# A gradient along rows: in-place tiles of one row per partition, six buffers, loads and stores in a fixed alternating order

## The chip, the cores and the metric

The kernel runs on one core of one Trainium2 chip; the other cores are idle. The metric is the device time of one execution in microseconds (us); less is better. All runs quoted here were in the fast state, with a granted clock of 1.0. A ratio is the mean time of one kernel's fast runs over the mean time of the fast runs of the kernel before from the same rounds, so it is not quite the ratio of the medians beside it. Ratios carry a 95% interval.

## The reference

```python
def setup_inputs():
    return {"x": np.random.randn(8192, 8192).astype(np.float32)}   # seeded

def reference(x):
    return np.gradient(x, axis=1)
```

Inside a row the result is `(x[j+1] - x[j-1]) / 2`; at its two ends it is the plain difference of neighbours. There is almost no arithmetic: 268.44 MB are read and 268.44 MB are written.

## The kernel before

A set is 256 rows, two consecutive rows for each of the 128 partitions of SBUF, the memory on the chip that the engines compute in. One load brings a set, 8 MB, into one of two buffers. Each of the two rows goes through a subtraction on VectorE (DVE) into an output tile, a multiplication by 0.5 on ScalarE (ACT), and a 4 MB store. All transfers are issued on the queue of SyncE (SP). The last set is cut into quarters, so that its first store can start early.

```python
    R = 2
    ...
    x_sets = x.rearrange("(s p t) m -> s p t m", p=P, t=R)
    out_sets = out.rearrange("(s p t) m -> s p t m", p=P, t=R)
    xpool = ctx.enter_context(tc.tile_pool(name="xpool", bufs=2))   # 2 x 64 KB per partition
    opool = ctx.enter_context(tc.tile_pool(name="opool", bufs=2))   # 2 x 32 KB per partition

    for i in range(nsets):                                          # 32 sets
        x_tile = xpool.tile([P, R, m], x.dtype)
        nc.sync.dma_start(out=x_tile, in_=x_sets[i])                # L32
        nchunks = 4 if i == nsets - 1 else 1
        for t in range(R):
            o_tile = opool.tile([P, m], out.dtype)
            for c in range(nchunks):
                ...
                nc.vector.tensor_sub(out=o_tile[:, lo:hi], ...)     # L45
                ...                                                 # first and last column
                nc.scalar.mul(out=o_tile[:, lo:hi], in_=o_tile[:, lo:hi], mul=0.5)          # L62
                nc.sync.dma_start(out=out_sets[i, :, t, c0:c1], in_=o_tile[:, c0:c1])       # L67
```

## Time and profile before

Three runs took 1255.21 us in the median (1253.86 to 1257.19). What matters of the profile:

| | kernel before |
|---|---|
| span of the profiled run | 1256.6 us |
| DMA engines, share of 40 slices | 9 tenths or more in 39 of them |
| mean rate, reads and writes together | 427 GB/s |
| DVE, ACT busy | 45%, 36% |

The lines come from the profile page: busy time by engine, the 40 slices, the chain that ended last, the two costliest groups (line, engine, operation, output<-input, count, busy us, mean ns, idle time before them), and the transfers with their median time from issue to landing.

```profile
DVE 565.4 (45%) x198; ACT 452.3 (36%) x71; POOL 0.2 (0%) x4
...
DMA  9999999999999999999999999999999999999997
GB/s 405 430 430 434 438 432 432 423 433 432 441 434 416 429 432 444 434 423 423 433 443 432 430 425 431 435 441 430 423 433 436 441 427 425 428 432 428 434 412 308
...
DMA 58%; DVE 23%; ACT 18%; issue 0%; DVEq 0%
...
L45 DVE TENSOR_TENSOR o_tile<-x_tile 128x8190 f32<-128x8190 f32 (+2 forms) x70 | 556.7, 7959 | 679.4 <-DMA out_dram<-o_tile 656.8
L62 ACT ACTIVATE o_tile<-o_tile 128x8190 f32<-128x8190 f32 (+2 forms) x70 | 451.0, 6443 | 793.6 <-DVE o_tile L45 793.6
...
out_dram<-o_tile SPq DMA_DIRECT2D x62, 4096.0 KB, 23.0
...
x_tile<-in_x_dram SPq DMA_DIRECT2D x32, 42.5
```

DVE stands idle for 679.4 us, nearly all of it waiting for stores to free an output tile. That looks like a cost, but the DMA row says otherwise: the transfer engines are busy throughout. A store lands 23.0 us after its issue, while moving 4 MB takes about 9.7 us; so when a store is issued, some 13 us of other work is still queued ahead of it. I call this number (landing time less transfer time) the queue ahead. It is a rough measure: a landing counts from the engine that ends last, so it also holds the lag of that engine and about a microsecond of start and completion.

Only at the end is there a weak place. The windows view gives, for stretches of 4 us, the busy time of DVE, ACT and POOL, the TensorE clock (of no use here), the DMA share and GB/s. Packets count where they start, so shares scatter around 1.

```profile
1220.00:1224.00 4.00, 0.00 (x0) 0.00 (x0) 0.00 (x0) 1.00 0.97 418
1224.00:1228.00 4.00, 1.96 (x1) 0.00 (x0) 0.00 (x0) 1.00 0.46 197
1228.00:1232.00 4.00, 4.00 (x4) 3.27 (x2) 0.00 (x0) 1.00 0.49 211
1232.00:1236.00 4.00, 3.36 (x4) 3.42 (x3) 0.00 (x0) 1.00 1.01 420
```

For about 7 us the DMA engines are half idle. The timeline (start, duration, engine and line) shows why: the last set's first subtraction waits for a store to free its output tile.

```profile
1226.04 2.29 DVE L45 TENSOR_TENSOR o_tile<-x_tile 128x2047 f32<-128x2047 f32 x1 [20.19 <-DMA out_dram<-o_tile]
```

The trace also records every DMA packet with start, duration and size, and I use sums of these records:

- **Nominal time**: every packet at its usual duration, 309 ns for 8 KB, 1213 ns for 32 KB, 2418 ns for 64 KB, summed and divided by 16 engines. For the kernel before it is 1240.4 us.
- **Stalls**: what packets took beyond that, divided by 16. Here 7.7 us, of which 6.4 us in the 64 KB packets, that is in the loads.
- **Idle at the end**: 16 less the number of data packets open, integrated over time and divided by 16, late in the run. Here 3.9 us in the hole and 3.1 us while the engines finish one after the other.
- **Spread**: for each transfer, the time from its first to its last completion count. The Trainium skill, page "DMA: Bandwidth & Descriptors", section "Why a DMA increments its semaphore by 16 and not by 1", says that a DMA runs on up to 16 engines that finish independently, and the semaphore counts them. The traces here agree: 16 counts arrive for each transfer.

### The profile page before, as it was taken

What the parts mean: (1) busy time and instruction counts of PE and PEld (TensorE: products, weight loads), DVE (VectorE), ACT (ScalarE), POOL (GpSimd) and SP (SyncE); (2) the same over time, 40 slices, a digit from 0 to 9 for tenths busy, and PEclk for the clock granted to TensorE, in tenths of its full rate; (3) what the DMA queues carried; (4) which work ended last, traced back from release to release, by engine and by line L of the source; (5) the groups of instructions that cost most, each with busy time, mean ns of one, the idle gap of its engine ahead of it and who ended that gap; (6) DMA issues with size and microseconds to landing.
All of it is one profiled execution on the core that took longest, in us unless ns stands there. A gap on an engine that the chain in (4) does not pass through costs nothing.

```text
span 1256.6 us, 670 instructions
## 1 busy us (share of the span) xinstructions
DVE 565.4 (45%) x198; ACT 452.3 (36%) x71; POOL 0.2 (0%) x4
## 2 busy tenths in 40 slices
DVE  2534553345533455334553345533455333554335
ACT  0434422344223442234422344223443234432244
POOL 0000000000000000000000000000000000000000
DMA  9999999999999999999999999999999999999997
GB/s 405 430 430 434 438 432 432 423 433 432 441 434 416 429 432 444 434 423 423 433 443 432 430 425 431 435 441 430 423 433 436 441 427 425 428 432 428 434 412 308
DMA packets 14693, 536.92 MB, mean 427 GB/s; under 512 B 1632, under 2 KB 1632, under 8 KB 1632
## 3 DMA queue, kind: packets, MB, share of 16 engines
q1 hardware_dynamic: 14688, 536.88, 99.4%
q14 instruction: 5, 0.04, 0.0%
HBM read 268.44 MB, written 268.44 MB: 427 GB/s over the span
## 4 chain that ended last, share of the span: by engine, by line
DMA 58%; DVE 23%; ACT 18%; issue 0%; DVEq 0%
DMA out_dram<-o_tile 57%; DVE o_tile L45 23%; ACT o_tile L62 18%; DMA x_tile<-in_x_dram 2%; DVEq L45 0%; DVE o_tile L57 0%; DVE o_tile L51 0%; DVEq L95 0%
## 5 line engine op out<-in xcount | busy, mean ns | idle before, releaser
L45 DVE TENSOR_TENSOR o_tile<-x_tile 128x8190 f32<-128x8190 f32 (+2 forms) x70 | 556.7, 7959 | 679.4 <-DMA out_dram<-o_tile 656.8
L62 ACT ACTIVATE o_tile<-o_tile 128x8190 f32<-128x8190 f32 (+2 forms) x70 | 451.0, 6443 | 793.6 <-DVE o_tile L45 793.6
L51 DVE TENSOR_TENSOR o_tile<-x_tile 128x1 f32<-128x1 f32 x64 | 9.8, 153 | 0.0
L57 DVE TENSOR_TENSOR o_tile<-x_tile 128x1 f32<-128x1 f32 x64 | 9.8, 153 | 0.0
L62 ACT ACT_TABLE_LOAD x1 | 1.3, 1283 | 0.7 <-PEq L84 0.7
L84 POOL MEMSET const-bfloat16-1.0<- 128x1 bf16 x1 | 0.1, 101 | 0.0
L84 POOL MEMSET const-uint8-127<- 128x1 uint8 x1 | 0.1, 101 | 0.0
L84 POOL MEMSET const-float32-0.0<- 128x1 f32 x1 | 0.1, 98 | 0.2 <-issue 0.2
L84 POOL MEMSET const-float32-1.0<- 128x1 f32 x1 | 0.1, 98 | 0.0
## 6 DMA issues: line engine op xcount, KB each, us to landing
out_dram<-o_tile SPq DMA_DIRECT2D x62, 4096.0 KB, 23.0
out_dram<-o_tile SPq DMA_DIRECT2D x8, 1024.0 KB, 8.1
x_tile<-in_x_dram SPq DMA_DIRECT2D x32, 42.5
```

The lines of the kernel that those rows point to most:

```text
L45: nc.vector.tensor_sub(out=o_tile[:, lo:hi], in0=x_tile[:, t, lo + 1 : hi + 1], in1=x_tile[:, t, lo - 1 : hi - 1],)
L51: nc.vector.tensor_sub(out=o_tile[:, 0:1], in0=x_tile[:, t, 1:2], in1=x_tile[:, t, 0:1],)
L57: nc.vector.tensor_sub(out=o_tile[:, m - 1 : m], in0=x_tile[:, t, m - 1 : m], in1=x_tile[:, t, m - 2 : m - 1],)
L62: nc.scalar.mul(out=o_tile[:, lo:hi], in_=o_tile[:, lo:hi], mul=0.5,)
L84: nc = _bacc.Bacc("TRN2", target_bir_lowering=False, num_devices=1)
```

## The change

Its intent: every tile is one row per partition (4 MB), computed in place, with the data loaded 64 elements above where the result goes. That makes room for six buffers. Loads run ahead in a fixed order that no scheduler alters: after store i comes load i+4, which waits for store i-2.

```diff
-    R = 2
+    R = 1
+    LAG, BACK = 6, 2
+    SH = 64
...
-    xpool = ctx.enter_context(tc.tile_pool(name="xpool", bufs=2))
-    opool = ctx.enter_context(tc.tile_pool(name="opool", bufs=2))
+    pool = ctx.enter_context(tc.tile_pool(name="pool", bufs=LAG))
...
+    def diff(b, c0, c1):
+        ...                                        # first and last column cut
+        nc.vector.tensor_sub(
+            out=b[:, lo:hi],
+            in0=b[:, SH + lo + 1 : SH + hi + 1],
+            in1=b[:, SH + lo - 1 : SH + hi - 1],
+        )
+        ...
+        nc.scalar.mul(out=b[:, lo:hi], in_=b[:, lo:hi], mul=0.5)
+    def load(i):
+        b = pool.tile([P, SH + W], x.dtype)
+        nc.sync.dma_start(out=b[:, SH : SH + W], in_=x_sets[i])
+        return b
+    with tc.manual_schedule():
+        held = [load(i) for i in range(LAG)]
+        for i in range(nsets):                     # 64 tiles
+            b = held[i]
+            last = i == nsets - 1
+            step = m // 4 if last else m // 2
+            for c0 in range(0, W, step):
+                diff(b, c0, c0 + step)
+                if last: ...                       # store this quarter
+            if not last:
+                nc.sync.dma_start(out=out_sets[i], in_=b[:, 0:W])
+            j = i - BACK
+            if j >= 0 and j + LAG < nsets:
+                held.append(load(j + LAG))
```

More of the change, by code (lines that the diff above doesn't have):

```diff
@@ L19 @@
     n, m = x.shape
-    R = 2
-    rows_per_set = P * R
-    nsets = n // rows_per_set
-    x_sets = x.rearrange("(s p t) m -> s p t m", p=P, t=R)
-    out_sets = out.rearrange("(s p t) m -> s p t m", p=P, t=R)
-    xpool = ctx.enter_context(tc.tile_pool(name="xpool", bufs=2))
-    opool = ctx.enter_context(tc.tile_pool(name="opool", bufs=2))
-    for i in range(nsets):
-        x_tile = xpool.tile([P, R, m], x.dtype)
-        nc.sync.dma_start(out=x_tile, in_=x_sets[i])
-        last = i == nsets - 1
-        nchunks = 4 if last else 1
-        for t in range(R):
-            o_tile = opool.tile([P, m], out.dtype)
-            csz = m // nchunks
-            for c in range(nchunks):
-                c0 = c * csz
-                c1 = c0 + csz
-                lo = max(c0, 1)
-                hi = min(c1, m - 1)
-                nc.vector.tensor_sub(
-                    out=o_tile[:, lo:hi],
-                    in0=x_tile[:, t, lo + 1 : hi + 1],
-                    in1=x_tile[:, t, lo - 1 : hi - 1],
-                )
-                if c0 == 0:
-                    nc.vector.tensor_sub(
-                        out=o_tile[:, 0:1],
-                        in0=x_tile[:, t, 1:2],
-                        in1=x_tile[:, t, 0:1],
-                    )
-                if c1 == m:
-                    nc.vector.tensor_sub(
-                        out=o_tile[:, m - 1 : m],
-                        in0=x_tile[:, t, m - 1 : m],
-                        in1=x_tile[:, t, m - 2 : m - 1],
-                    )
-                nc.scalar.mul(
-                    out=o_tile[:, lo:hi],
-                    in_=o_tile[:, lo:hi],
-                    mul=0.5,
-                )
-                nc.sync.dma_start(
-                    out=out_sets[i, :, t, c0:c1], in_=o_tile[:, c0:c1]
-                )
@@ new lines @@
+    R = 1
+    LAG, BACK = 6, 2
+    SH = 64
+    W = R * m
+    nsets = n // (P * R)
+    x_sets = x.rearrange("(s p t) m -> s p (t m)", p=P, t=R)
+    out_sets = out.rearrange("(s p t) m -> s p (t m)", p=P, t=R)
+    pool = ctx.enter_context(tc.tile_pool(name="pool", bufs=LAG))
+    def diff(b, c0, c1):
+        lo, hi = c0, c1
+        if c0 % m == 0:
+            lo = c0 + 1
+            nc.vector.tensor_sub(
+                out=b[:, c0:lo],
+                in0=b[:, SH + c0 + 1 : SH + c0 + 2],
+                in1=b[:, SH + c0 : SH + c0 + 1],
+            )
+        if c1 % m == 0:
+            hi = c1 - 1
+        nc.vector.tensor_sub(
+            out=b[:, lo:hi],
+            in0=b[:, SH + lo + 1 : SH + hi + 1],
+            in1=b[:, SH + lo - 1 : SH + hi - 1],
+        )
+        if hi < c1:
+            nc.vector.tensor_sub(
+                out=b[:, hi:c1],
+                in0=b[:, SH + hi : SH + c1],
+                in1=b[:, SH + hi - 1 : SH + c1 - 1],
+            )
+        nc.scalar.mul(out=b[:, lo:hi], in_=b[:, lo:hi], mul=0.5)
@@ new lines, in load @@
+    def load(i):
[10 more added lines that the diff above has]
+                diff(b, c0, c0 + step)
+                if last:
+                    nc.sync.dma_start(
+                        out=out_sets[i, :, c0 : c0 + step], in_=b[:, c0 : c0 + step]
+                    )
+            if not last:
[3 more added lines that the diff above has]
+                held.append(load(j + LAG))
```

## The prediction

> **What bounds the kernel now.** The DMA engines. The page's DMA row is 9 in every one of 40 slices but the last (7), at a mean of 427 GB/s over 1256.6 us. DVE is busy 45%, ACT 36%. The chain of waits names stores (58%), L45 (23%) and L62 (18%), but that is the chain through small buffer pools, not idle DMA: DVE waits 656.8 us for stores while the queue still holds work. Counting the trace's packet records, 16 are open at every moment from first to last data packet, except near the end.
>
> The packets' durations give the ceiling: 64 KB in 2418 ns, 32 KB in 1213, 8 KB in 309: 27.2 GB/s per engine plus about 8 ns a packet, or 432 to 434 GB/s on 16 engines. The Trainium skill, page "DMA: Bandwidth & Descriptors", section "Where 436 GB/s comes from", states 435.2 GB/s as the fabric's ceiling; this trace agrees within 1%. 536.87 MB must move either way. To be had are only:
> - stalls of packets beyond these durations: 7.7 us per engine, 6.4 of them in 64 KB loads;
> - a hole before the last set, whose compute waits for a store (20.2 us at 1226 us): some 9 engines idle for 6.5 us, 3.7 us on average;
> - an uneven end, about 3 us on average (one engine ends 3.7 us after most);
> - start and completion, 1.7 us each.
>
> **What the change does.**
> - Loads become 4 MB in 32 KB rows: 4096 packets of 64 KB become 8192. Estimate from the durations: +8 ns x 4096 / 16 = +2.1 us; fewer 8 KB packets at the end give back 0.3 to 0.5.
> - The first compute starts after 4 MB (about 11 us, not 22.5). Worth nothing: the queue is full of loads then.
> - Load i+4 waits only for store i-2, with about four transfers of 9.7 us queued behind that store (before, 14 to 24 us of queue were left). As the queue never ran dry, no gain in the steady part.
> - At the end, stores 60 to 62 (29 us) follow load 63 and hide the last tile's compute. The hole goes; but the lagging engines, which set the end, hardly waited in it: 0.5 to 3.5 us gained.
> - DVE and ACT work in halves (about 4.4 and 3.6 us): 12.4 us a tile from landing to result, against 19.4 us of DMA per tile. Hidden.
>
> **Sum.** +1.7 for packets, -0.5 to -3.5 at the end, stalls as before: about 1 us less. I predict 1254 us, range 1248 to 1260; within 2% 0.95; faster by over 2% 0.02 (the data alone take about 1238 us); slower by over 2% 0.03.
>
> **What would show it.**
> - DMA row 9 to the end, mean 427 to 431 GB/s; the last two slices above 412 and 308; 32 KB packets still at about 1213 ns.
> - No hole before the last tile.
> - DVE's waits for stores replaced by waits for loads, 650 to 690 us in total, worth nothing. Loads take about 50 us to land, stores 50 to 56 (before 42.5 and 23): a deeper queue.
> - DVE and ACT busy as before within 3%.
>
> **What would make it wrong.** Loads and stores alternate every 4 MB instead of 8, and a deep queue lets engines drift apart: if mixed reads and writes stall packets more often, the 7.7 us grow (conceivably 1 to 2% slower); if 32 KB rows stall less, they shrink by up to 6 us. An engine that lags more, or less, moves the uneven end by a few us.

## The result, and the profile after

The changed kernel took 1252.07 us in the median (1251.22 to 1252.39, 4 runs) beside 1256.2 us for the kernel before in all its runs up to then (1253.86 to 1257.59, 4 runs). The ratio is 0.9968 (0.9949 to 0.9987): about 4 us, or 0.3%, faster. The same parts of the page:

```profile
DVE 587.1 (47%) x258; ACT 464.5 (37%) x131; POOL 0.2 (0%) x4
...
DMA  9999999999999999999999999999999999999998
GB/s 403 422 434 436 434 430 430 430 433 431 432 432 432 434 429 434 433 431 435 432 430 436 431 434 433 433 433 433 432 436 431 434 432 431 436 434 430 435 431 350
...
DMA 63%; another core or an unknown queue 18%; DVE 12%; ACT 5%; SPq 0%; issue 0%; DVEq 0%
...
L58 ACT ACTIVATE b<-b 128x4095 f32<-128x4095 f32 (+1 forms) x130 | 463.2, 3563 | 743.6 <-DVE b L47 743.6
L47 DVE TENSOR_TENSOR b<-b 128x4095 f32<-128x4095 f32 (+1 forms) x130 | 566.7, 4359 | 4.8 <-DVE b L40 0.3
L40 DVE TENSOR_TENSOR b<-b 128x1 f32<-128x1 f32 x64 | 10.2, 160 | 625.2 <-DMA b<-in_x_dram 625.2
...
b<-in_x_dram SPq DMA_DIRECT2D x64, 4096.0 KB, 48.4
out_dram<-b SPq DMA_DIRECT2D x63, 4096.0 KB, 55.0
```

DVE now waits for loads (625.2 us) and not for stores, and that is worth as little as before: its wait changed its name, not the time. A store lands 55.0 us after its issue, so the queue ahead of it grew from 13 to 45 us. (The 18% of the chain on "an unknown queue" are steps that this view could not attribute; nothing is read from it.) The GB/s row is more even: before, it swings between 416 and 444 in the steady part, now between 429 and 436 from the third slice on. The windows at the end:

```profile
1228.00:1232.00 4.00, 0.00 (x0) 0.00 (x0) 0.00 (x0) 1.00 0.97 418
...
1236.00:1240.00 4.00, 0.00 (x0) 0.00 (x0) 0.00 (x0) 1.00 0.98 414
1240.00:1244.00 4.00, 0.00 (x0) 0.00 (x0) 0.00 (x0) 1.00 0.81 340
1244.00:1248.00 4.00, 0.00 (x0) 0.00 (x0) 0.00 (x0) 1.00 0.19 82
```

The hole is gone; what is left is a ragged end, in which fewer and fewer engines have work. The sums over packet records, two profiles of each kernel (the second ones are the controls below):

| | before | before again | after | after again |
|---|---|---|---|---|
| span, us | 1256.6 | 1254.3 | 1249.4 | 1250.5 |
| data packets | 13056 | 13056 | 16768 | 16768 |
| nominal time, us | 1240.4 | 1240.4 | 1242.3 | 1242.3 |
| stalls, us per engine | 7.7 | 6.0 | 2.7 | 2.5 |
| idle, hole + ragged end, us | 3.9 + 3.1 | 3.4 + 3.0 | 0.0 + 3.9 | 0.0 + 5.1 |
| spread, us, at 300 / 600 / 1100 us | 5.1 / 8.9 / 11.7 | 3.5 / 6.4 / 10.0 | 4.1 / 5.5 / 5.5 | 5.5 / 6.5 / 6.5 |

(Spreads are means over the 100 us that begin there.) The mean span fell by 5.5 us. Stalls fell by 4.3 us (mean of 7.7 and 6.0, less that of 2.7 and 2.5). Idle time at the end fell by 2.2 us (6.7 to 4.5). The smaller packets cost 1.9 us of nominal time, of which 0.7 us come back: a packet can start a few ns before the one before it on its engine ends, and the packets open beyond 16, integrated over time and divided by 16, rose from 2.6 to 3.3 us. Start and completion took 0.3 us less, and small gaps in the middle of the run 0.1 us more. That makes -4.3 - 2.2 + 1.9 - 0.7 - 0.3 + 0.1 = -5.5 us. The largest term is the stalls, which the prediction had left "as before". (Over all 43 times of before and the nine of the changed kernel the means are 1255.8 and 1251.8 us, 4 us apart. The first profile of before fell on a slow execution: time and span differ by 1.8 us in the other runs, so its time was about 1258.4 us by this estimate, and only five of the 43 took longer. So the terms hold for these profiles, and on average their sum is smaller.)

The spread goes with it: before, the engines drift apart all the time, while some keep stalling; after, they drift for some 500 us, then nearly keep their distances (5.5 us from first to last in every later transfer of the first profile). In the changed kernel 1.4 of the 2.6 us of stalls fall into the first 100 us and almost none after 600 us.

### The profile page after: what moved, and what is told of

Its sections match the earlier page's. It is cut to its first block, busy times and chain, and to the rows that moved or that the text cites. A ratio compares the mean times of both kernels' runs of the same rounds, so it can differ in the third digit from the quotient of the medians.

```text
span 1249.4 us, 813 instructions
## 1 busy us (share of the span) xinstructions
DVE 587.1 (47%) x258; ACT 464.5 (37%) x131; POOL 0.2 (0%) x4
## 4 chain that ended last, share of the span: by engine, by line
DMA 63%; another core or an unknown queue 18%; DVE 12%; ACT 5%; SPq 0%; issue 0%; DVEq 0%
DMA b<-in_x_dram 59%; DVE b L47 11%; ACT b L58 5%; DMA out_dram<-b 4%; SPq L80 0%; DVE b L40 0%; DVEq L40 0%; SPq L62 0%
## 5 line engine op out<-in xcount | busy, mean ns | idle before, releaser
L58 ACT ACTIVATE b<-b 128x4095 f32<-128x4095 f32 (+1 forms) x130 | 463.2, 3563 | 743.6 <-DVE b L47 743.6
L47 DVE TENSOR_TENSOR b<-b 128x4095 f32<-128x4095 f32 (+1 forms) x130 | 566.7, 4359 | 4.8 <-DVE b L40 0.3
L40 DVE TENSOR_TENSOR b<-b 128x1 f32<-128x1 f32 x64 | 10.2, 160 | 625.2 <-DMA b<-in_x_dram 625.2
L53 DVE TENSOR_TENSOR b<-b 128x1 f32<-128x1 f32 x64 | 10.2, 159 | 2.2
## 6 DMA issues: line engine op xcount, KB each, us to landing
b<-in_x_dram SPq DMA_DIRECT2D x64, 4096.0 KB, 48.4
out_dram<-b SPq DMA_DIRECT2D x4, 1024.0 KB, 27.1
```

The costliest lines, as they stand in the source:

```text
L40: nc.vector.tensor_sub(out=b[:, c0:lo], in0=b[:, SH + c0 + 1 : SH + c0 + 2], in1=b[:, SH + c0 : SH + c0 + 1],)
L47: nc.vector.tensor_sub(out=b[:, lo:hi], in0=b[:, SH + lo + 1 : SH + hi + 1], in1=b[:, SH + lo - 1 : SH + hi - 1],)
L53: nc.vector.tensor_sub(out=b[:, hi:c1], in0=b[:, SH + hi : SH + c1], in1=b[:, SH + hi - 1 : SH + c1 - 1],)
L58: nc.scalar.mul(out=b[:, lo:hi], in_=b[:, lo:hi], mul=0.5)
```

## Experiments

Two theories at first. Theory A: the gain is fewer stalls, from smaller load packets or from the new order. Theory B: stalls are noise of single profiles and the gain is the hole. Theories C to G came with the later results. Every kernel gave correct results, and all were timed in five rounds beside the kernel before.

### Controls: both kernels again

No edit.

> The kernel before, unchanged, as a control. A second profile says how much the stalls (packet time beyond 2418, 1213 and 309 ns: 7.7 us per engine in the first profile) and the span (1256.6 us) vary from one execution to the next. Theory A (the 64 KB loads stall more than 32 KB loads): again 6 to 9 us of stalls, nearly all in 64 KB packets. Theory B (stalls are noise of single executions and the gain is the hole before the last set): stalls may come out anywhere from 2 to 9 us. Both: ratio 1.000 within 0.002; the hole of about 6 us on about 9 engines is there again.

> The changed kernel, unchanged, for a tight ratio and a second profile. First ratio 0.9968 (0.9949 to 0.9987). Both theories: ratio 0.995 to 0.998. Theory A: stalls again 2 to 4 us per engine (2.7 in the first profile). Theory B: stalls as scattered as those of the control, up to 8 us.

The kernel before: ratio 1.0005 (0.9988 to 1.0022), stalls 6.0 us, 5.7 of them in the 64 KB packets. The changed kernel: 1251.58 us, ratio 0.9964 (0.9947 to 0.9982), stalls 2.5 us. So the stalls are a property of the kernels and not of one profile, and a ratio near 1.000 or 0.996 can be told apart from the other. A side result: in these rounds the kernel before scattered from 1251.94 to 1258.95 us, the changed one from 1251.22 to 1252.26 us.

### Take away the hole alone

The last set is computed in place in its input tile, so its compute waits for no store; all else stays.

```diff
+            if last:
+                o_tile, to = x_tile, t * m  # in place, SH below the input
+            else:
+                o_tile, to = opool.tile([P, m], out.dtype, name="o_tile"), 0
```

> The kernel before with only its last set in place, so that the last set's compute waits for no store. The hole of 3.7 us on average before the last set must be gone in the packet records. Theory B (the hole is the gain): about 1252.5 us, ratio 0.9970, as the changed kernel. Theory A (fewer stalls are the gain, the lagging engines that set the end did not wait in the hole): within 1 us of before, ratio 0.999 to 1.000; stalls stay at 6 to 9 us.

1256.65 us, ratio 1.0001 (0.9981 to 1.0021). The hole is filled, as the windows of this kernel show against those of before:

```profile
1224.00:1228.00 4.00, 3.90 (x5) 2.78 (x3) 0.00 (x0) 1.00 1.01 430
1228.00:1232.00 4.00, 3.96 (x2) 3.38 (x2) 0.00 (x0) 1.00 0.98 416
...
1240.00:1244.00 4.00, 0.00 (x0) 0.00 (x0) 0.00 (x0) 1.00 0.83 350
1244.00:1248.00 4.00, 0.00 (x0) 0.00 (x0) 0.00 (x0) 1.00 0.41 174
1248.00:1252.00 4.00, 0.00 (x0) 0.00 (x0) 0.00 (x0) 1.00 0.32 135
```

Yet no gain shows: the idle time moved from the hole to the ragged end (0.0 + 7.5 us in place of 3.9 + 3.1). The engines that ended late had not run dry in the hole; only those that were ahead had, and they now wait at the end. With a spread of 11.4 us, a hole of 7 us costs the late engines nothing. Theory B, which asked for 0.9970, falls; a gain of 1 or 2 us would not show in this interval.

### Smaller packets alone

The rows of the input tile are padded by 64 elements in SBUF, so that the same 8 MB loads go in 32 KB packets.

```diff
-        x_tile = xpool.tile([P, R, m], x.dtype)
-        nc.sync.dma_start(out=x_tile, in_=x_sets[i])
+        x_tile = xpool.tile([P, R, m + 64], x.dtype)
+        nc.sync.dma_start(out=x_tile[:, :, 0:m], in_=x_sets[i])
```

> The kernel before with x_tile's rows padded by 64 elements, so that the same 8 MB loads go in packets of 32 KB and all else stays. Packets of 2418 ns become pairs of 1213 ns: +2.1 us by themselves. Theory A with packet size as the cause of stalls: stalls fall from 7.7 to about 3 us per engine, time about 3 us shorter, ratio 0.997 to 0.999. Theory B, or stalls that come from 8 MB phases and not from packet size: stalls as in the control, time 1 to 3 us longer, ratio 1.001 to 1.002.

1255.58 us, ratio 0.9996 (0.9978 to 1.0014). Stalls were 4.3 us: fewer than in either profile of before, but not the 3 that the packet size was to explain. The time expected from this did not come either: some 2.6 us of stalls were saved on the mean (6.9 to 4.3), and 2.1 us of nominal time were paid for twice as many load packets. The spread still grew to 9.0 us. Packet size is a part of the answer, and in the time it cancels itself.

### Finer loads, and a surprise

Each 8 MB load is split into two of 4 MB; the tiles and pools stay.

```diff
-        nc.sync.dma_start(out=x_tile, in_=x_sets[i])
+        for t in range(R):
+            nc.sync.dma_start(out=x_tile[:, t, :], in_=x_sets[i, :, t, :])
```

> The kernel before, with each 8 MB load split into two 4 MB loads, one per row of a partition: 32 KB packets, and 4 MB loads and stores in alternation, but separate tiles and 2+2 buffers as before. Padding alone left stalls of 4.3 us per engine (before 7.7 and 6.0, changed 2.7 and 2.5). Theory C (what is left is the finer alternation of loads and stores): stalls 2.3 to 3 us, ratio about 0.998 (the hole stays). Theory D (it is the deep queue, which lets engines drift apart): stalls 3.8 to 4.5 us, ratio 0.999 to 1.000, as in the padded kernel.

1295.84 us, ratio 1.0316 (1.0288 to 1.0344). Both theories missed by far: stalls were 42.5 us, and 10.2 us of idle time lay in the middle of the run. The scheduler had used the finer transfers to reorder the queue: load, store, load, store, in place of a set's load and then its two stores. From this kernel's page:

```profile
GB/s 399 430 429 433 419 410 425 411 403 420 408 429 405 414 416 415 419 403 419 420 405 419 418 406 420 405 431 406 416 407 413 427 403 413 410 409 415 419 417 344
...
out_dram<-o_tile SPq DMA_DIRECT2D x62, 4096.0 KB, 14.0
```

And from its timeline:

```profile
617.75 7.03 ACT L63 ACTIVATE o_tile<-o_tile 128x8190 f32<-128x8190 f32 x1 [14.19 <-DVE o_tile L46]
624.80 0.33 SPq L68 DMA_DIRECT2D out_dram<-o_tile  x1
625.23 0.38 SPq L33 DMA_DIRECT2D x_tile<-in_x_dram  x1
628.64 8.69 DVE L46 TENSOR_TENSOR o_tile<-x_tile 128x8190 f32<-128x8190 f32 x1 [10.79 <-DMA x_tile<-in_x_dram]
```

The queue issues in order. A load now stands behind a store that waits for ACT, though the load's own buffer is free by then: ACT ends at 624.78, the store goes at 624.80, the load at 625.23. The Trainium skill, page "DMA: Bandwidth & Descriptors", section "Anatomy of one DMA — SWDGE (gpsimd) path", says that DMA engines do not wait on semaphores; the wait happens on the issuing sequencer. That is what these lines show, here for the SP queue: one waiting store holds back everything behind it. A store lands after 14.0 us, so some 4 us are ahead of it by the measure above, and the packet records show that hardly any of it is queued work: the load before ends on 15 engines at 625.0 to 625.4 us, and the store issued at 624.80 begins on them at 625.6. In the microsecond that begins at 634 us, 15 of the 16 packets that start are stalled, by 11.2 us together. They are the last packets of that store: they end at 635.9 to 636.5 us, where the engines' 4-byte semaphore packets for the store start, and the load's packets follow. So nearly all engines reach the end of the store, and turn to the load, at once. Summed over the run, 27.8 of the 42.5 us were lost while 15 or more packets were stalled at the same instant (packets over 0.1 us late, each counted at the middle of its time).

### Where the rows lie in memory

The changed kernel with its rows dealt out so that neighbouring partitions are 64 KB apart in memory, as in the kernel before, and not 32 KB.

```diff
-    x_sets = x.rearrange("(s p t) m -> s p (t m)", p=P, t=R)
+    x_sets = x.rearrange("(s p t) m -> s t p m", p=P, t=2)     # used as x_sets[i // 2, i % 2]
```

(The output likewise.)

> The changed kernel with the rows dealt out so that neighbouring partitions read and write every other row of memory: the same 32 KB packets, DMAs and order, but 64 KB from one partition's row to the next in memory, as in the kernel before. Theory E (the 64 KB pitch is part of the stalls): stalls rise from 2.6 to 3.5 us or more. Theories C and D: stalls 2.3 to 3 us, ratio 0.995 to 0.998 as the changed kernel.

1251.3 us, ratio 0.9957 (0.9941 to 0.9974), stalls 3.4 us. The stalls are a little higher than 2.7 and 2.5, just short of what theory E asked for, but the time is no worse than that of the changed kernel. Theory E explains no time.

### Large packets in the changed kernel

Two rows per partition, three buffers of 64 KB, all else as changed: 8 MB loads and stores in 64 KB packets.

```diff
-    R = 1
-    LAG, BACK = 6, 2
+    R = 2
+    LAG, BACK = 3, 1
```

> The changed kernel with two rows per partition and 3 buffers of 64 KB: in place, fixed order and deep queue stay; loads and stores become 8 MB in 64 KB packets. Half the packets: 8 ns times 8000 / 16, 4 us less by itself. Theory D (the deep queue cuts the stalls): stalls 2.5 to 3.5 us, ratio 0.993 to 0.995, the fastest so far. Packet size or coarse alternation makes the stalls: 6 to 8 us or more, ratio 0.996 to 1.000.

1249.59 us, ratio 0.9945 (0.9928 to 0.9961), the fastest. Nominal time 1238.4 us (3.9 less than the changed kernel's), stalls 4.6 us (2.0 more). So large packets and large transfers do stall more, but not as in the kernel before: here the stalls die away, with 0.1 us or less per 100 us from 900 us on, while the kernel before loses some 0.2 to 0.7 us in almost every 100 us to the end. The spread settles at 6.5 us.

### Half the queue

Four buffers in place of six, load i+3 after store i.

```diff
-    LAG, BACK = 6, 2
+    LAG, BACK = 4, 1
```

> The changed kernel with 4 buffers in place of 6 and load i+3 after store i: about 20 us of queue behind the store that a load waits for, in place of 39. Theory D (depth and drift matter): stalls rise to 3.5 us or more, late in the run too; ratio 0.997 to 1.000. Theory C (fine alternation and packet size are enough): stalls 2.3 to 3 us, ratio 0.995 to 0.998.

1252.22 us, ratio 0.9965 (0.9946 to 0.9983), stalls 3.1 us. A store lands after 35.6 us (26 us ahead). Two of the six buffers buy nothing: theory D is wrong at this depth.

### The order alone

The split loads of the slow kernel, with the issue order written out: both stores of a set, then both loads.

```diff
+    def load(i):
+        x_tile = xpool.tile([P, R, m], x.dtype)
+        for t in range(R):
+            nc.sync.dma_start(out=x_tile[:, t, :], in_=x_sets[i, :, t, :])
+        return x_tile
+    ctx.enter_context(tc.manual_schedule())
+    held = [load(0), load(1)]
...
+        if i + 2 < nsets:
+            held.append(load(i + 2))       # after both stores of set i
```

> The split-load kernel that came out 3.2% slower (stalls 42 us per engine, and 14 us of engines standing idle), with only the issue order on the queue put back to that of before: both stores of a set, then both 4 MB loads. Theory F (the split let the scheduler put each store in front of the next load, the queue ran dry every set, all engines then turn from writes to reads in the same microsecond and stall some 0.75 us each time): stalls back to 4 to 5 us as in the padded kernel, no idle in the steady part, ratio 0.998 to 1.001. Theory G (4 MB loads, or two DMAs into one tile, stall by themselves): stalls stay above 20 us, ratio above 1.015.

1254.11 us, ratio 1.0000 (0.9982 to 1.0018); stalls 4.8 us. A store lands after 23.0 us again. The same tiles, the same transfers and the same packets: the order on the queue was the whole 3.2%. Theory G falls.

### Not in place

The changed kernel with four input tiles and two output tiles, the same SBUF, load i+4 after store i.

```diff
-    LAG, BACK = 6, 2
+    LAG, BACK = 4, 0
+    opool = ctx.enter_context(tc.tile_pool(name="opool", bufs=2))
...
+            o = opool.tile([P, W], x.dtype)   # diff() writes o, stores read o
```

> The changed kernel not in place: 4 input tiles and 2 output tiles of the same 32 KB rows (the same SBUF), load i+4 after store i. The queue keeps about 17 us ahead by an estimate from 9.7 us per transfer. Theory F (queue depth and drift of the engines decide, in place is only a means): stalls 2.3 to 4 us, ratio 0.995 to 0.999. If in place itself matters (separate tiles as in the slow split kernel): stalls above 10 us, ratio above 1.01.

1256.08 us, ratio 1.0014 (0.9996 to 1.0033). The stalls came as expected, 3.6 us, and died away; the time missed, and the trace shows why, first in the windows, then in the timeline:

```profile
1224.00:1228.00 4.00, 3.69 (x2) 3.33 (x2) 0.00 (x0) 1.00 0.30 131
1228.00:1232.00 4.00, 3.54 (x3) 4.00 (x2) 0.00 (x0) 1.00 0.01 2
```

```profile
1218.80 0.16 DVE L41 TENSOR_TENSOR o<-b 128x1 f32<-128x1 f32 x1 [10.40 <-DMA out_dram<-o]
...
1228.46 0.16 DVE L41 TENSOR_TENSOR o<-b 128x1 f32<-128x1 f32 x1 [0.76 <-DMA out_dram<-o]
```

The next-to-last tile's compute at 1218.80 and the last one's at 1228.46 each had to wait until a store freed an output tile, and no load was left to fill the queue meanwhile. The hole is now 6.9 us of idle per engine, and for some us all 16 engines are idle: the spread is only 4.8 us, so the hole reaches the late engines as well. This is what in place buys here: the last tiles need no output tile.

### A queue that is too short

Three buffers, load i+2 after store i.

```diff
-    LAG, BACK = 6, 2
+    LAG, BACK = 3, 1
```

> The changed kernel with 3 buffers and load i+2 after store i: by an estimate from 9.7 us per transfer and 12.4 us of compute per tile the queue falls to about 5 us, or runs dry, once per tile. Theory F: engines are held together, stalls do not die away in the course of the run; stalls 6 to 40 us per engine, ratio 1.002 to 1.03. If depth is without effect: stalls 2.3 to 3 us, ratio 0.995 to 0.998.

1275.94 us, ratio 1.0170 (1.0147 to 1.0194). Stalls 26.7 us, at some 2 us in nearly every 100 us to the end. Theory F's numbers hold, and one edit brought it about; the kernel with four buffers above, which does not lose, differs from this one in a single number (LAG 4 or 3). From this kernel's page:

```profile
GB/s 395 427 434 429 425 436 429 425 420 425 427 419 426 426 427 424 418 427 427 428 413 426 426 422 419 420 422 424 422 419 428 417 419 428 427 412 427 425 420 338
...
out_dram<-b SPq DMA_DIRECT2D x63, 4096.0 KB, 16.8
```

A store lands after 16.8 us, 7 us ahead. The DMA engines are almost never idle before the end (1.4 us per engine over 1050 us), so this loss does not show as an empty DMA row: it shows in longer packets. One part of theory F is not confirmed. Here mostly 4 to 11 engines stall at once, not all 16, and the spread is 5.0 us, as in the changed kernel, which does not stall.

### A version that beats both

Two rows per partition, three buffers, and the last set in halves.

```diff
-    R = 1
-    LAG, BACK = 6, 2
+    R = 2
+    LAG, BACK = 3, 1
...
-            step = m // 4 if last else m // 2
+            step = m // 2
```

> A version to beat both: the changed kernel with two rows per partition and 3 buffers (ratio 0.9945, 1249.6 us in the run before), and the last set in halves of 16 KB packets in place of quarters of 8 KB (8 ns times 512 / 16, 0.3 us less; its compute is hidden by stores that still wait in the queue). Expected: 1249 us, ratio 0.993 to 0.996; stalls 4 to 5 us.

1249.59 us, ratio 0.9963 (0.9944 to 0.9981), stalls 4.8 us. The kernel before was faster in these rounds (1253.62 us in the median; 1257.7 in those of the first version), so the ratio is poorer than 0.9945 at the same time. The two sets of rounds ran on different chips (0 and 3), the repeat of the changed kernel on a third (5). By the times themselves: all 12 runs of the two versions with two rows lie between 1248.09 and 1250.67 us, all nine of the changed kernel between 1251.22 and 1252.39 us. That is about 2 us, or 0.2%. On one and the same chip (3) the changed kernel itself was not timed, but its variant with the 64 KB pitch was, and it took 1250.64 to 1252.03 us beside 1248.95 to 1250.67. The halves in place of quarters added nothing that shows.

### All together

Queue ahead is a store's median landing time less 9.7 us (19.4 us for 8 MB). Stalls are those after the first 100 us.

| kernel | queue ahead, us | stalls after 100 us | ratio |
|---|---|---|---|
| split loads, scheduler's order | 4 | 40.9 | 1.0316 |
| changed, three buffers | 7 | 24.6 | 1.0170 |
| before (two profiles) | 13 | 6.3, 4.5 | 1.0005 |
| before, hole filled | 13 | 5.1 | 1.0001 |
| before, padded rows | 13 | 3.2 | 0.9996 |
| split loads, order of before | 13 | 3.0 | 1.0000 |
| changed, not in place | 16 | 1.8 | 1.0014 |
| changed, two rows | 17 | 2.7 | 0.9945 |
| changed, two rows, last set in halves | 17 | 3.1 | 0.9963 |
| changed, four buffers | 26 | 1.4 | 0.9965 |
| changed, 64 KB pitch | 45 | 1.7 | 0.9957 |
| changed (two profiles) | 45 | 1.3, 1.1 | 0.9964 |

With 4 and 7 us ahead, stalls cost 2 to 3%. From 13 us up they differ by a few us, and packet size, order and the hole count as much as depth. No run lies between 7 and 13 us, so where the loss sets in is not known.

## Why the prediction was right or wrong

The time was right: 1254 us predicted, 1252.07 us measured, within 1248 to 1260, and within 2% as given 0.95. That says little of the mechanism: the range would have held no change as well, and the gain that the sum forecast, about 1 us, is a quarter of the 4 us measured. Point by point:

- *The DMA engines are the bound, and only a few us are to be had.* Right. The DMA row is full in all kernels here, and the fastest is 0.4 to 0.6% below before.
- *+2.1 us for smaller load packets.* Right as nominal time (+1.9 with the shorter last tile); 0.7 us of it comes back, since packets on one engine overlap by a few ns.
- *The hole goes, for 0.5 to 3.5 us.* The hole went, and the reason for the low end ("the lagging engines, which set the end, hardly waited in it") held: taken away alone, the hole was worth nothing that shows (1.0001, 0.9981 to 1.0021). What did fall at the end, 2.2 us of idle time, goes with a smaller spread.
- *As the queue never ran dry, no gain in the steady part; stalls as before.* This step failed. The largest term of the gain is in the steady part: stalls fell from 6.9 to 2.6 us per engine. The prediction named this way out ("if 32 KB rows stall less, they shrink by up to 6 us"), but booked it at zero, and packet size is only a part of it: padding alone went to 4.3 us. The rest goes with the fine alternation and the longer queue together; the runs don't divide it cleanly. (After the first 100 us, split loads in the old order left 3.0 us of stalls, padding 3.2, and fine alternation behind 16 us of queue 1.8: a hint at the alternation, no more.)
- *A deep queue lets engines drift apart, which might cost 1 to 2%.* The opposite held. In the changed kernel the engines come to rest at fixed distances and stop stalling; it is with a short queue that the kernel stalls and comes out 1.7 to 3.2% slower.
- *DVE's waits for loads, 650 to 690 us; DVE and ACT busy as before within 3%.* Slightly off: 625.2 us, because DVE was busy 587.1 us and not 565.4 (3.8% more). Loads at 48.4 us and stores at 55.0 us to landing were as predicted, as were 430 GB/s and the last two slices (431 and 350).

What stays open is why a short queue makes packets stall. Where they stall can be read from the records, since each engine ends its share of a transfer with a semaphore packet. At most one data packet in eight is the last one of its share (it ends within 8 ns of the start of a semaphore packet), but 33.9 of the 42.5 us of the slowest kernel lie in these last packets, 16.4 of 26.7 with three buffers, and 6.4 of 7.7 in the kernel before. So stalls belong to the hand-over from one transfer to the next. In the slowest kernel 15 of the engines reach it within 1 us of each other (median from 300 us on) and stall there together. In the one with three buffers it is 10, and groups of 4 to 11 stall; but in the changed kernel it is 11 or 12, and these hardly stall at all. So engines that hand over together are a suspect, shown in one kernel and not in the others. Nor is it a turn to reading alone: before, 6.4 of the 7.7 us lay in the packets of the loads.

## What to carry to other kernels

In this copy-like kernel with full DMA engines, changing the waits of the compute engines gained nothing; look at how long packets take against their usual duration, and at how far the engines' completions lie apart. Keep transfers queued ahead of every store on an in-order queue: here 13 us and more were enough, 4 and 7 us were not. Check the issue order when transfers are split, and fix it by hand if need be: a scheduler's reordering alone cost 3.2% here. A hole near the end cost nothing that shows where the engines lay 11 us apart, and showed in the time where they lay 4.8 us apart; so compare the two before mending a hole.

## What the Trainium skill lacked or had wrong

- "DMA: Bandwidth & Descriptors", section "Where 436 GB/s comes from", gives 435.2 GB/s and says that for transfers between HBM and SBUF the HBM side (about 358) binds. With the other cores idle it did not: 27.1 GB/s per engine in 64 KB packets (65536 B in 2418 ns), 433.7 GB/s on 16, and 430 GB/s over the whole changed kernel, half of it writes. The section itself notes a measurement of 425, and elsewhere the skill gives about 358 as the share of a core when both cores of a pair stream; the sentence lacks that condition.
- "SBUF — State Buffer", section "Summary: rules for kernel authors", advises about 358 GB/s for estimates of such transfers. With that figure this kernel would be estimated at 1500 us (536.87 MB / 358 GB/s); it takes 1252. This rule, too, does not say that it is for two busy cores.
- No page tells of packets that stall when little is queued: 24.6 to 40.9 us per engine with 4 to 7 us queued ahead, 1.1 to 1.7 us with 26 or more (after the first 100 us), with the DMA row full in both cases. Nor does any tell that the stalls lie mostly in the last packets of a transfer (33.9 of 42.5 us in the slowest kernel).
- No page tells how far the 16 engines of one core drift apart on equal work (beyond saying that they finish independently, and that two of them are usually slower in traces): up to 11.7 us here, which sets the end of the kernel.
- The rule for authors in the DMA page, "≥1 MiB per DMA", does not reach this far: at 4 MB and 8 MB per transfer the issue order still made 3.2%.
